# Encoder trunk on one core: first norm and first weight splits taken off GpSimd, and a scheduler that models transfers

## The chip, the core and the metric

The kernel runs on one core of one Trainium2 chip. Its engines run beside one another, each with its own queue, in order: TensorE (PE, matrix products, transposes by a product with the identity), VectorE (DVE), ScalarE (ACT), GpSimd (POOL) and SyncE (SP), which here issues all DMA transfers. The metric is the device time of one execution in microseconds; less is better.

## The reference

A trunk of two layers over 528 positions (16 meta tokens and 512 frames; pads in front stay zero), model width 1024, float32:

```python
for layer in range(DEPTH):
    hn = rms_norm(h, norm_g[layer])
    if layer % 2 == 0:   # A: sparse attention on top-k keys; B: gated linear attention
        out = layer_ab(hn, ...)
    else:                # C: retention with rotary; D: stick-breaking attention
        out = layer_cd(hn, ...)
    h = h + where(valid, out, 0)
return rms_norm(h[frames], final_g)

def rms_norm(x, g):
    return x * rsqrt(mean(x * x, -1) + 1e-6) * g
```

`layer_ab` begins with one projection of `hn` by `w_in_ab`, whose columns give the queries, keys, values and gates of A and B and the indexer (its queries IQ, its key, weights and B's low-rank gate); the indexer's scores pick 128 keys for each query. Each layer ends with a projection by `w_out_*`.

## The kernel before

Every float32 product is made from three products of split operands: an operand x is split into a high part (`hi`, written by ScalarE as fp32r) and the rest (`lo`, a subtraction, on VectorE). hh and hl are the split, normalised, transposed activations, 8 tiles of 128 features by 528 positions; wh and wl are a split weight tile, raw the tile as loaded (256 KB each, half of the rows of 128 columns). `products` issues hh x wh, hl x wh and hh x wl for each feature tile k, in two column halves of 272 (meta tokens and blocks 0 and 1) and 256 (blocks 2 and 3).

The head is `load_x` (lines 709 to 784). It loads the meta tokens (two halves x0 and x1 of 512 features, gv) and four blocks of 128 frames (x0 and x1, pt), the gains (mid) and five raw weights; IQ's two come first, then the two of the combined columns COMB (indexer key, indexer weights and low-rank gate, loaded in three pieces each into a zeroed tile). `square` adds up the squares, x0 on ScalarE and x1 on VectorE; `norm` makes the reciprocal root on ScalarE (`rstd`, two instructions) and scales x0 on VectorE and x1 on GpSimd (line 750). `turn` transposes one feature tile of a group of blocks on TensorE and writes hh (ScalarE, with the gain) and hl (VectorE). `split_next` (line 562) splits the next raw: of the first PW tiles the wh, and of the first PL tiles the wl, is GpSimd's (line 482: PW = 2, PL = 1). `consts` keeps TensorE at work before with 46 transposes of the identity.

No instruction goes straight to its engine. Each one is recorded (`Recorder.add`), with what it depends on and a cost in ns by `price`. `deadlines` then goes through all of them from the end and gives each the latest time at which it may begin for TensorE's order to hold; this is its priority (`pri`). `order` walks through time: on each engine, of the instructions that can start earliest, it takes the one with the least `pri`, and so sets the order of all five queues, and with it which buffers come free when. For VectorE it knows a collision: an instruction with both operands in SBUF (`port`) that starts while a GpSimd instruction runs is stretched to the end of that. A transfer's cost is a fixed 2000 and a share by its size, with any number of transfers side by side.

In the middle of the first layer the two head groups are worked between the projections: top-k (MAX and MATCH_REPLACE on VectorE over lt tiles of 272, 400 or 528 columns), GLA (st, vm, attm, the mask applied to the meta tokens' scores, used at lines 1324 to 1346), and softmax (wt, y).

Of the kernel before, what the change touches and what calls it, by code (L numbers as in the profile page):

```python
# [13 lines left out]
ALU = mybir.AluOpType  # L14
# [152 lines left out]
class Recorder:  # L167
# [48 lines left out]
    def price(self, o):  # L216
        o.mm, o.port = None, False
        n = max([x.free() for x in o.ins + o.outs] or [1])
        sbuf = not any(x.tile.psum for x in o.ins)
        scalar = 65 if any(isinstance(x, View) and x.free() == 1 for x in o.ins) and n > 1 else 0  # L220
        if o.eng == "tensor":
            lhs, rhs = (o.args[1], o.args[2]) if len(o.args) > 2 else (o.kw["lhsT"], o.kw["rhs"])
            turn = o.name == "transpose"
            plain = rhs.dtype == F32
            k, m, n = lhs.shape[0], lhs.free(), rhs.free()
            two = plain and not turn
            o.mm = (k, plain, max(n * 0.455 * (2 if two else 1) + 4, 107 * m / P + 4) + (107 if two and n <= P else 0))
            o.cost = max(273, 170 + 0.4375 * n) if not two else 180 + 1.62 * n
        elif o.eng == "scalar":
            o.cost = (205 if sbuf else 165) + 0.83 * n + (80 if isinstance(o.kw.get("bias"), View) or isinstance(o.kw.get("scale"), View) else 0)  # L230
            if "accum_out" in o.kw:
                o.cost += 200
        elif o.eng == "vector":
            o.port = sbuf and o.name not in ("max", "match_replace")
            if o.name == "tensor_tensor_scan":
                o.cost = 144 + 2.1 * n
            elif o.name in ("tensor_scalar", "tensor_copy") and sbuf:
                o.cost = 160 + 0.52 * n + scalar
            elif o.name == "memset":
                o.cost = 100 + 0.3 * n  # L240
            else:
                o.cost = 148 + 1.05 * n + scalar
            if o.name == "tensor_tensor_reduce" or "accum_out" in o.kw:
                o.cost += 80
            if o.name == "match_replace":
                o.cost += 70
        elif o.eng == "gpsimd":
            o.cost = {"memset": 92 + 0.84 * n, "tensor_tensor": 178 + 2.17 * n}.get(o.name, 194 + 1.5 * n)
        else:
            x = o.outs[0] if o.outs else o.ins[0]  # L250
            kb = n * x.shape[0] / 256
            o.cost = 2000 + kb * (9 if any(y.tile.whole for y in o.outs + o.ins) else 3.5)


    LAT = {"tensor": 55, "vector": 33, "scalar": 34, "gpsimd": 60, "sync": 27}
# [4 lines left out]
    def deadlines(self):  # L260


        ops, t, last = self.ops, 0.0, None
        due = {}
        for o in ops:
            if o.eng == "tensor":
                if last is not None:
                    t += self.slot(last, o)
                last = o
            due[o] = t  # L270
        late = {}
        turn = {}
        for o in reversed(ops):
            end = min([late[q] - self.LAT[q.eng] for q in o.succs] + [late[q] - self.LAT[q.eng] for x in o.tiles
                      for q in [turn.get((x.kind, x.at + x.kind.bufs))] if q and q.at > o.at], default=due[o] + 20000)
            start = end - o.cost
            if o.eng == "tensor":
                start = min(start, due[o])
            late[o] = start
            for x in o.tiles:  # L280
                turn[x.kind, x.at] = o
        for o in ops:
            o.pri = due[o] if o.eng == "tensor" else late[o]

    def order(self):
        ops = self.ops
# [5 lines left out]
        ends = {}  # L292
        free = dict.fromkeys(self.LAT, 0.0)
        lists = {e: [] for e in self.LAT}
        last = None
        begun = {}
        result = []

# [15 lines left out]
        while left:  # L314
            best = None
            for e, xs in lists.items():
                pick = None
                base = free[e] + (last.mm[2] if e == "tensor" and last is not None else 0)
                for o in xs:
                    est = o.est  # L320
                    ok = True
                    for t in o.tiles:
                        if t.slot:
                            continue
                        k = t.kind
                        if t.at != k.next or not k.free:
                            ok = False
                            break
                        est = max(est, min(k.free)[0] + self.LAT[e])
                    if not ok:  # L330
                        continue
                    now = free[e] + (self.slot(last, o) if e == "tensor" and last is not None else 0)
                    start = max(est, now)
                    key = (max(est + (self.MARGIN if e == "tensor" else 0) - base, 0.0), o.pri)
                    if pick is None or key < pick[0]:
                        pick = (key, start, o)
                if pick and (best is None or pick[1] < best[1]):
                    best = pick
            assert best, "no instruction can be placed"
            _, start, o = best  # L340
            e = o.eng
            lists[e].remove(o)
            cost = o.cost
            if e == "vector" and o.port and begun.get("pool", (0, 0))[0] < start < begun.get("pool", (0, 0))[1] - 100:
                cost += begun["pool"][1] - start - 70
            end = start + cost
            ends[o] = end
            o.begin, o.end = start, end
            if e == "tensor":
                free[e], last = start, o  # L350
            elif e == "sync":
                free[e] = start + 430
            else:
                free[e] = end + self.OVER[e]
                if e == "gpsimd":
                    begun["pool"] = (start, end)
# [40 lines left out]
class Kernel:  # L397
# [81 lines left out]
    LASTK = 4  # L479


    XL, XC, XN, XW, PW, PL = 2, 9, (0, 1, 1, 2), (1, 4, 7, 10, 13), 2, 1
    WARM = 46

    LAG = {"a": 5, "d": 6, "t": 1, "v": 4, "n": 9, "s": 6, "k": 11}
# [223 lines left out]
    def load_x(self):  # L709
        nc, ins = self.nc, self.ins  # L710
# [4 lines left out]
        for b in (None, 0, 1, 2, 3):  # L715
            n = NMETA if b is None else P
# [27 lines left out]
        def norm(b):  # L744
            n = NMETA if b is None else P
            x0, x1 = xs[b]
            r = ms[b][:n]
            self.rstd(r, r, DM)
            nc.vector.tensor_scalar(x0[:n], x0[:n], r, None, op0=ALU.mult)
            nc.gpsimd.tensor_scalar(x1[:n], x1[:n], r, 1.0, op0=ALU.mult, op1=ALU.mult)  # L750

        def turn(group, t0, k):
            tr = self.s()
# [13 lines left out]
        for b in first:  # L767
            square(b)
            norm(b)
# [640 lines left out]
    def out_ab(self):  # L1410
# [8 lines left out]
        rx = [self.wt() for _ in range(KT)]  # L1419
        halves = self.HALVES  # L1420
        begin = lambda f: self.begin(w, P * f, self.mh, self.ml, order=order)

        def residual(f):
# [369 lines left out]
```

## Time and profile before

| | |
|---|---|
| median of 3 runs | 663.05 us (662.98 to 663.65) |
| the profiled execution | 663.46 us |
| its span | 661.7 us |
| mean granted clock of TensorE | 0.984 |
| HBM traffic | 53.18 MB read, 6.90 MB written, 91 GB/s over the span |
| largest group of ScalarE, wh<-raw, x152 | 94.7 us, 629 ns each |
| largest group of VectorE, wl<-raw,wh, x153 | 109.1 us, 718 ns each |

Times in the profile are microseconds from the span's start. The span is what lies between the first and the last recorded instruction; the time of the execution has a little more around it. Idle time of an engine is put down to what ended it, in brackets as [time <- what]. A helper records every operation, so all have one line, L393 (in the changed kernel L403), and are told apart by tile names.

### The profile page before, as it was taken

To read this page: it belongs to the slowest core of one execution; us is meant where nothing else is said; L and a number is where in the kernel's file an instruction comes from. 1 tells how busy PE (TensorE), PEld (TensorE's weight loads), DVE (VectorE), ACT (ScalarE), POOL (GpSimd) and SP (SyncE) were. 2 spreads that over 40 slices of the span, in tenths; PEclk is the share of its full clock that TensorE was granted. 3 is DMA by queue.
4 is the path that set the end of the run, shared out by engine and by line. 5 is a ranking of instruction groups with operands and counts; after the bars stand their busy time and mean duration, and the time that the engine had idled before them with its cause. 6 is when DMAs were issued, how large, how long until landed. Compare 5 with 4: busy or idle time off the path is not lost.

```text
span 661.7 us, 12217 instructions
## 1 busy us (share of the span) xinstructions
PE 636.6 (96%) x4469; PEld 581.4 (88%) x4469; DVE 484.3 (73%) x1176; ACT 405.1 (61%) x910; POOL 76.4 (12%) x124
## 2 busy tenths in 40 slices
PE   5999999899999999999999999999999999999996
PEld 5879989798899999999899999878988888988884
DVE  4777799899987869679632764699935699955643
ACT  3656563353444877699643675799744699944434
POOL 7101110111000000001121110001200001110030
PEclk8899999799999999999999999999999999999998
DMA  7437222132322323112143272203322203224403
GB/s 217 118 83 224 72 74 72 46 96 65 81 57 75 98 65 97 52 47 65 50 145 112 67 238 81 64 21 93 97 65 64 78 2 104 83 71 149 153 17 127
DMA packets 91104, 59.25 MB, mean 90 GB/s; under 512 B 7315, under 2 KB 81629, under 8 KB 91045
## 3 DMA queue, kind: packets, MB, share of 16 engines
q1 hardware_dynamic: 91044, 58.48, 30.8%
q8 instruction: 35, 0.57, 0.3%
q14 instruction: 25, 0.20, 0.1%
HBM read 53.18 MB, written 6.90 MB: 91 GB/s over the span
## 4 chain that ended last, share of the span: by engine, by line
PE 67%; DVE 18%; ACT 9%; issue 2%; DMA 2%; SPq 0%; DVEq 0%; ACTq 0%
PE acc L393 45%; PE x L393 15%; PE y L393 6%; ACT wt L393 6%; DVE wt L393 5%; DVE st L393 3%; DVE lt L393 3%; DVE wl L393 3%; DVE m L393 2%; DMA pt<-in_x_dram 2%; ACT pt L393 1%; DVE pt L393 1%; ACT ptm L393 1%; ACT st L393 0%; DVE vt L393 0%
## 5 line engine op out<-in xcount | busy, mean ns | idle before, releaser
L393 PE MATMUL acc<-hh,wh 128*128 128x272 f32 (+2 forms) x968 | 246.5, 315 | 3.0 <-ACT hh L393 1.5
L393 PE MATMUL acc<-hh,wl 128*128 128x272 f32 (+2 forms) x968 | 234.2, 302 | 1.9 <-DVE wl L393 1.9
L393 PE MATMUL acc<-hl,wh 128*128 128x272 f32 (+2 forms) x968 | 234.8, 304 | 0.7 <-DVE hl L393 0.5
L393 ACT ACTIVATE wh<-raw 128x512 fp32r<-128x512 f32 x152 | 94.7, 629 | 125.2 <-PE acc L393 110.6
L393 PEld LDWEIGHTS acc<-hh,wh 128*128 128x128 f32 x968 | 159.5, 190 | 10.2 <-issue 3.0
L393 PEld LDWEIGHTS acc<-hh,wl 128*128 128x128 f32 x968 | 158.2, 190 | 8.5 <-DVE wl L393 2.8
L393 PEld LDWEIGHTS acc<-hl,wh 128*128 128x128 f32 x968 | 158.2, 190 | 5.0 <-DVE hl L393 1.5
L393 DVE TENSOR_TENSOR wl<-raw,wh 128x512 fp32r<-128x512 f32 x153 | 109.1, 718 | 57.2 <-ACT wh L393 52.2
L393 ACT ACTIVATE wt<-x 128x272 f32<-128x272 f32 (+3 forms) x100 | 43.0, 453 | 28.4 <-PE x L393 17.8
L393 POOL TENSOR_TENSOR gt<-gt,wt 128x528 f32<-128x528 f32 (+1 forms) x16 | 21.2, 1326 | 322.5 <-ACT wt L393 303.4
L393 PE MATMUL x<-st,st 128*128 128x272 f32 (+6 forms) x240 | 51.5, 292 | 0.1
L393 PE MATMUL x<-ident,wt 128*128 128x128 f32 (+2 forms) x300 | 46.0, 275 | 2.1 <-DVE wt L393 1.2
L393 ACT ACTIVATE wt<-wt 128x528 f32<-128x528 f32 (+3 forms) x74 | 42.9, 603 | 4.7 <-DVE wt L393 4.0
L393 PEld LDWEIGHTS x<-st,st 128*128 128x128 f32 (+2 forms) x240 | 37.5, 185 | 8.8 <-ACT wt L393 3.1
L393 ACT ACTIVATE wt<-wt,tiny 128x272 f32<-128x272 f32 (+5 forms) x64 | 34.7, 561 | 10.3 <-DVE tiny L393 10.0
L393 PEld LDWEIGHTS x<-ident,wt 128*128 128x128 f32 (+2 forms) x300 | 33.7, 139 | 7.0 <-DVE pt L393 1.4
L393 PE MATMUL y<-pt,vt 128*128 128x256 f32 (+1 forms) x288 | 38.6, 277 | 0.0
L393 PEld LDWEIGHTS y<-pt,vt 128*128 128x128 f32 x288 | 36.4, 189 | 1.3 <-DVE pt L393 0.7
L393 ACT ACTIVATE st<-acc 64x528 fp32r<-64x528 f32 (+1 forms) x58 | 34.7, 599 | 1.1 <-DVE lt L393 0.5
L393 DVE TENSOR_TENSOR_SCAN wt<-wt,wt 128x64 f32<-128x64 f32 (+5 forms) x50 | 30.8, 654 | 1.5 <-ACT wt L393 1.3
L393 DVE TENSOR_TENSOR pt<-x,pt 128x384 fp32r<-128x384 f32 (+1 forms) x48 | 28.1, 594 | 2.7 <-ACT pt L393 2.1
L393 ACT ACTIVATE wt<-wt,one 128x528 f32<-128x528 f32 (+3 forms) x42 | 29.5, 705 | 0.2
(191 smaller groups left out, 893.9 us busy)
## 6 DMA issues: line engine op xcount, KB each, us to landing
raw<-in_w_in_ab_dram SPq DMA_DIRECT2D x64, 256.0 KB, 2.8
raw<-in_w_in_cd_dram SPq DMA_DIRECT2D x56, 256.0 KB, 2.9
raw<-in_w_out_ab_dram SPq DMA_DIRECT2D x16, 256.0 KB, 2.8
raw<-in_w_out_cd_dram SPq DMA_DIRECT2D x16, 256.0 KB, 2.6
rep<-rows SPq DMA_DIRECT2D x8, 328.0 KB, 6.8
lt<-rep SPq DMA_DIRECT2D x8, 264.0 KB, 3.0
pt<-in_x_dram SPq DMA_DIRECT2D x8, 256.0 KB, 5.2
wt<-in_x_dram SPq DMA_DIRECT2D x8, 256.0 KB, 3.3
```

The lines of the kernel that those rows point to most:

```text
L393: getattr(getattr(self.core, o.eng), o.name)(*[bind(x) for x in o.args], **{k: bind(x) for k, x in o.kw.items()})
```

## The change

GpSimd's part of the first norm goes to VectorE, and the first two wh and the first wl go to ScalarE and VectorE (PW = PL = 0). The other parts are in the scheduler. A transfer now costs 3.6 ns per KB and takes its turn on one common wire: it ends when the wire is free, but not before 1900 ns after its issue, plus this cost; a transfer from DRAM to DRAM ends 6900 ns after its issue. Transfers get as priority the place at which the program asks for them (`o.at`) in place of the latest time, which is reckoned with 3000 ns more. And a GpSimd instruction that starts while a VectorE one with both operands in SBUF runs is stretched as well.

```diff
--- before.py
+++ after.py
@@ -249,7 +249,7 @@
         else:
             x = o.outs[0] if o.outs else o.ins[0]
             kb = n * x.shape[0] / 256
-            o.cost = 2000 + kb * (9 if any(y.tile.whole for y in o.outs + o.ins) else 3.5)
+            o.cost = kb * 3.6
 
 
     LAT = {"tensor": 55, "vector": 33, "scalar": 34, "gpsimd": 60, "sync": 27}
@@ -273,14 +273,14 @@
         for o in reversed(ops):
             end = min([late[q] - self.LAT[q.eng] for q in o.succs] + [late[q] - self.LAT[q.eng] for x in o.tiles
                       for q in [turn.get((x.kind, x.at + x.kind.bufs))] if q and q.at > o.at], default=due[o] + 20000)
-            start = end - o.cost
+            start = end - o.cost - (3000 if o.eng == "sync" else 0)
             if o.eng == "tensor":
                 start = min(start, due[o])
             late[o] = start
             for x in o.tiles:
                 turn[x.kind, x.at] = o
         for o in ops:
-            o.pri = due[o] if o.eng == "tensor" else late[o]
+            o.pri = due[o] if o.eng == "tensor" else o.at if o.eng == "sync" else late[o]
 
     def order(self):
         ops = self.ops
@@ -293,6 +293,7 @@
         free = dict.fromkeys(self.LAT, 0.0)
         lists = {e: [] for e in self.LAT}
         last = None
+        wire = 0.0
         begun = {}
         result = []
 
@@ -331,7 +332,8 @@
                         continue
                     now = free[e] + (self.slot(last, o) if e == "tensor" and last is not None else 0)
                     start = max(est, now)
-                    key = (max(est + (self.MARGIN if e == "tensor" else 0) - base, 0.0), o.pri)
+                    pri = o.pri
+                    key = (max(est + (self.MARGIN if e == "tensor" else 0) - base, 0.0), pri)
                     if pick is None or key < pick[0]:
                         pick = (key, start, o)
                 if pick and (best is None or pick[1] < best[1]):
@@ -343,13 +345,21 @@
             cost = o.cost
             if e == "vector" and o.port and begun.get("pool", (0, 0))[0] < start < begun.get("pool", (0, 0))[1] - 100:
                 cost += begun["pool"][1] - start - 70
+            if e == "gpsimd" and begun.get("port", (0, 0))[0] < start < begun.get("port", (0, 0))[1] - 100:
+                cost += begun["port"][1] - start - 100
             end = start + cost
+            if e == "vector" and o.port:
+                begun["port"] = (start, end)
             ends[o] = end
             o.begin, o.end = start, end
             if e == "tensor":
                 free[e], last = start, o
             elif e == "sync":
                 free[e] = start + 430
+                wire = end = max(wire, start + 1900) + o.cost
+                if o.outs and o.outs[0].tile.whole and o.ins and o.ins[0].tile.whole:
+                    end = start + 6900
+                ends[o] = o.end = end
             else:
                 free[e] = end + self.OVER[e]
                 if e == "gpsimd":
@@ -479,7 +489,7 @@
     LASTK = 4
 
 
-    XL, XC, XN, XW, PW, PL = 2, 9, (0, 1, 1, 2), (1, 4, 7, 10, 13), 2, 1
+    XL, XC, XN, XW, PW, PL = 2, 9, (0, 1, 1, 2), (1, 4, 7, 10, 13), 0, 0
     WARM = 46
 
     LAG = {"a": 5, "d": 6, "t": 1, "v": 4, "n": 9, "s": 6, "k": 11}
@@ -747,7 +757,7 @@
             r = ms[b][:n]
             self.rstd(r, r, DM)
             nc.vector.tensor_scalar(x0[:n], x0[:n], r, None, op0=ALU.mult)
-            nc.gpsimd.tensor_scalar(x1[:n], x1[:n], r, 1.0, op0=ALU.mult, op1=ALU.mult)
+            nc.vector.tensor_scalar(x1[:n], x1[:n], r, None, op0=ALU.mult)
 
         def turn(group, t0, k):
             tr = self.s()
```

What this does to the queues is shown at three places.

SyncE, the first transfers of the program (gv: meta tokens, pt: blocks of x, mid: gains, raw: weights). Before:

```order
1 L393 DMA pt_144<-in_x_dram 128x512
2 L393 DMA pt_157<-in_x_dram 128x512
3 L393 DMA pt_167<-in_x_dram 128x512
4 L393 DMA pt_177<-in_x_dram 128x512
5 L393 DMA gv_185<-in_meta_tokens_dram 16x512
6 L393 DMA gv_196<-in_meta_tokens_dram 16x512
7 L393 DMA raw_202<-in_w_in_ab_dram 128x4x128
8 L393 DMA mid_208<-in_norm_g_dram 16x128
9 L393 DMA mid_208<-in_gla_gate_b_dram 2x128
10 L393 DMA raw_224<-in_w_in_ab_dram 128x4x128
11 L393 DMA pt_234<-in_x_dram 128x512
12 L393 DMA raw_227<-in_w_in_ab_dram 128x4x64
```

Now:

```order
1 L403 DMA gv_144<-in_meta_tokens_dram 16x512
2 L403 DMA gv_157<-in_meta_tokens_dram 16x512
3 L403 DMA pt_167<-in_x_dram 128x512
4 L403 DMA pt_177<-in_x_dram 128x512
5 L403 DMA pt_185<-in_x_dram 128x512
6 L403 DMA pt_199<-in_x_dram 128x512
7 L403 DMA mid_207<-in_norm_g_dram 16x128
8 L403 DMA mid_207<-in_gla_gate_b_dram 2x128
9 L403 DMA raw_220<-in_w_in_ab_dram 128x4x128
10 L403 DMA raw_230<-in_w_in_ab_dram 128x4x128
11 L403 DMA pt_238<-in_x_dram 128x512
12 L403 DMA pt_250<-in_x_dram 128x512
```

The meta tokens stand ahead of the x blocks, both IQ weights (128x4x128) ahead of blocks 2 and 3, and the first piece of COMB (128x4x64) behind all of x, at row 15; its last two pieces (128x4x16), rows 23 and 27 before, are at rows 31 and 32.

ScalarE, its first instructions (wt, tiny: a square with its sum; tiny<-tiny: the two halves of a reciprocal root; wh: a weight's high part; hh: a transposed tile's high part). Before:

```order
6 L393 COPY gains<-x_257 128x18
7 L393 ACTIVATE wt_272,tiny_273<-pt_167 128x512
8 L393 ACTIVATE tiny_270<-tiny_270,eps 128x1
9 L393 ACTIVATE tiny_270<-tiny_270 128x1
10 L393 ACTIVATE wt_301,tiny_302<-pt_234 128x512
11 L393 ACTIVATE tiny_299<-tiny_299,eps 128x1
12 L393 ACTIVATE tiny_299<-tiny_299 128x1
13 L393 ACTIVATE wh_318<-raw_227 128x512
14 L393 ACTIVATE hh_327<-x_277,gains 128x272
15 L393 ACTIVATE hh_327<-x_279,gains 128x272
16 L393 ACTIVATE hh_327<-x_281,gains 128x272
```

Now:

```order
6 L403 ACTIVATE wt_264,tiny_265<-pt_185 128x512
7 L403 ACTIVATE tiny_262<-tiny_262,eps 128x1
8 L403 ACTIVATE tiny_262<-tiny_262 128x1
9 L403 COPY gains<-x_268 128x18
10 L403 ACTIVATE wh_285<-raw_220 128x512
11 L403 ACTIVATE tiny_289<-tiny_289,eps 128x1
12 L403 ACTIVATE tiny_289<-tiny_289 128x1
13 L403 ACTIVATE wh_298<-raw_230 128x512
14 L403 ACTIVATE wt_305,tiny_306<-pt_238 128x512
15 L403 ACTIVATE hh_316<-x_271,gains 128x272
16 L403 ACTIVATE hh_316<-x_275,gains 128x272
```

The wh ahead of the first hh was the first of COMB (raw_227); now the two of IQ stand there (raw_220, raw_230), and the wh of COMB are behind the thirteenth hh. The meta tokens' and block 0's squares and their roots, ahead of these rows, keep their order.

VectorE, in the top-k of the first layer (MAX and MATCH_REPLACE over lt; the wt<-y,tiny further on is a normalised attention output that TensorE transposes next). Before, with that wt at row 277:

```order
260 L393 MATCH_REPLACE lt_646<-m_35_1960,lt_646 128x400
261 L393 SCALAR_TENSOR_TENSOR st_1997<-st_1997,lt_1378,x_2029 64x128
262 L393 MATCH_REPLACE lt_635<-m_34_1930,lt_635 128x272
263 L393 SCALAR_TENSOR_TENSOR st_1997<-st_1997,lt_1378,x_2029 64x128
264 L393 MAX m_37_2137<-lt_635 128x8
265 L393 MAX m_38_2144<-lt_646 128x8
266 L393 MAX m_39_2151<-lt_687 128x8
267 L393 SCALAR_TENSOR_TENSOR st_2009<-acc_2058,wt_2027 64x4x64 x2
268 L393 SCALAR_TENSOR_TENSOR st_2023<-acc_2058,wt_2034 64x4x64 x2
269 L393 SCALAR_TENSOR_TENSOR st_2031<-acc_2058,wt_2027 64x4x64 x2
270 L393 SCALAR_TENSOR_TENSOR st_2041<-acc_2058,wt_2034 64x4x64 x2
```

Now, around that wt, at row 281:

```order
279 L403 TENSOR_REDUCE tiny_2195<-wt_2153 128x4
280 L403 TENSOR_TENSOR wl_2201<-raw_1867,wh_2144 128x512
281 L403 TENSOR_TENSOR wt_2210<-y_1930,tiny_2195 128x512
282 L403 TENSOR_TENSOR wl_2219<-raw_1937,wh_2185 128x512
283 L403 MAX m_38_2227<-lt_646 128x8
284 L403 MAX m_39_2238<-lt_687 128x8
285 L403 TENSOR_TENSOR mx_1934<-x_2225,gt_1921 128x512
286 L403 TENSOR_TENSOR wl_2255<-raw_2030,wh_2232 128x512
```

Before, all three MAX of this round (m_37, m_38 and m_39) stood ahead of it; now only m_37 does, at row 270, and the two of 400 and 528 columns (lt_646 and lt_687) come behind it. On the other hand the MAX of lt_646 of the round before (m_35), which stood at row 238, is now at row 260, still ahead of it.

Of GpSimd's rows eight go (two wh, one wl, five norms). VectorE gains six rows of these, ScalarE two. On TensorE no instruction is added or removed; rows move in the head and at some ten places behind it.

## The prediction

> **What bounds the kernel now.** I read the engines' shares and the granted clock in the page first, then TensorE's timeline for every idle stretch, then the chain and the timelines of the engines that TensorE waits for.
>
> ```profile
> span 661.7 us, 12217 instructions
> PE 636.6 (96%) x4469; PEld 581.4 (88%) x4469; DVE 484.3 (73%) x1176; ACT 405.1 (61%) x910; POOL 76.4 (12%) x124
> PEclk8899999799999999999999999999999999999998
> ```
>
> TensorE (PE) is busy for 96% of the span, so 661.7 - 636.6 = 25.1 us are idle. The matrix work isn't changed; time can come only from idle stretches or from stretches at a lower clock. The clock row has two low places, the first two slices (0 to 33 us) and the eighth (116 to 132 us). The profiled execution took 663.46 us, 1.76 more than its span. TensorE's timeline of the start, in order of time (start, length, what; in brackets the idle time before and who ended it):
>
> ```profile
> 1.59 7.31 PE L393 MATMUL y<-ident 128*128 128x128 f32 x46 [1.59 <-POOL ident masks.py:199]
> 9.63 0.35 PE L393 MATMUL x<-ident,gv 16*128 16x16 f32 x3 [0.57 <-DVE gv L393]
> 12.38 0.65 PE L393 MATMUL x<-ident,pt 128*128 128x128 f32 x3 [2.40 <-DVE pt L393]
> 14.96 0.90 PE L393 MATMUL x<-ident,pt 128*128 128x128 f32 x3 [1.93 <-DVE pt L393]
> 17.38 0.79 PE L393 MATMUL acc<-hh,wh 128*128 128x272 f32 x2 [1.52 <-ACT hh L393]
> 36.04 0.40 PE L393 MATMUL acc<-hh,wh 128*128 128x512 f32 x1
> ```
>
> After 46 warming transposes TensorE waits for VectorE's normalised x (pt) twice, and starts its first product at 17.38. 36.04 is the first product of the second column group, my mark for the end of the head. The clock in stretches (busy times of PE, PEld, DVE, ACT, POOL, then the clock, DMA share, GB/s):
>
> ```profile
> 12.00:13.00 1.00, 0.62 (x3) 0.31 (x3) 1.00 (x3) 0.09 (x1) 1.00 (x3) 0.84 1.11 349
> 13.00:22.00 9.00, 5.55 (x21) 4.13 (x20) 6.95 (x15) 5.23 (x14) 2.72 (x7) 0.50 0.80 191
> 22.00:23.00 1.00, 1.00 (x6) 0.96 (x7) 0.88 (x2) 0.23 (x1) 0.00 (x0) 0.54 0.00 0
> 23.00:36.00 13.00, 13.00 (x107) 12.64 (x107) 9.12 (x18) 8.16 (x18) 0.99 (x1) 1.00 0.31 78
> 122.00:128.00 6.00, 6.00 (x26) 5.02 (x26) 4.51 (x12) 0.76 (x3) 1.30 (x2) 0.50 0.18 44
> ```
>
> The clock is halved from about 12.7 to 22.9 (a mean of 0.84 from 12 to 13 and of 0.54 from 22 to 23), and again from 122 to beyond 128. It came back about 5.5 us after the products had begun at 17.38. What stands ahead of 17.38, by the chain of waits and by ScalarE's (ACT), VectorE's (DVE) and GpSimd's (POOL) timelines:
>
> ```profile
> 2.13 4.76 DMA pt<-in_x_dram
> ...
> 8.41 5.51 DMA pt<-in_x_dram
> ...
> 13.94 2.19 DMA raw<-in_w_in_ab_dram
> ...
> 16.23 0.63 ACT wh L393
> 16.86 0.39 ACT hh L393
> ```
> ```profile
> 7.14 0.63 ACT L393 ACTIVATE wt<-gv 16x512 f32<-16x512 f32 x1 [5.11 <-DMA gv<-in_meta_tokens_dram]
> 16.23 0.63 ACT L393 ACTIVATE wh<-raw 128x512 fp32r<-128x512 f32 x1 [2.79 <-DMA raw<-in_w_in_ab_dram]
> 10.34 1.99 DVE L393 TENSOR_SCALAR pt<-pt,tiny 128x512 f32<-128x512 f32 x1
> 13.48 1.43 DVE L393 TENSOR_SCALAR pt<-pt,tiny 128x512 f32<-128x512 f32 x1
> 19.34 1.15 DVE L393 TENSOR_SCALAR pt<-pt,tiny 128x512 f32<-128x512 f32 x1
> 23.70 0.48 DVE L393 TENSOR_SCALAR pt<-pt,tiny 128x512 f32<-128x512 f32 x1
> 16.89 0.69 DVE L393 TENSOR_TENSOR wl<-raw,wh 128x512 fp32r<-128x512 f32 x1 [1.32 <-ACT wh L393]
> 9.16 1.65 POOL L393 TENSOR_SCALAR gv<-gv,tiny 16x512 f32<-16x512 f32 x1 [0.65 <-DVE wt L393]
> 7.80 0.71 POOL L393 TENSOR_SCALAR wh<-raw 128x512 fp32r<-128x512 f32 x1 [1.02 <-DMA raw<-in_w_in_ab_dram]
> ```
>
> Three things hold the head. ScalarE and VectorE begin with the meta tokens (gv), which land at 7.1 behind four blocks of x. VectorE's norm takes 0.48 us at 23.70 and 1.15 to 1.99 us while GpSimd works. And ScalarE stands 2.79 us before a split of the combined weights (COMB), whose third piece of DMA lands at 16.13, with the first hh queued behind it.
>
> **The change part by part.**
>
> The norm and the splits. GpSimd loses eight instructions: five x1 norms, two wh, one wl. VectorE gains five norms of 0.48 us and one wl of 0.69, 3.1 us in all. In the head it is rid of the collisions, (1.99 - 0.48) + (1.43 - 0.48) + (1.15 - 0.48) = 3.1 us: VectorE's sum is even. TensorE's first transposes need x0 of the meta tokens and of blocks 0 and 1. Of the five x1 norms only that of the meta tokens stands ahead of the last of these on VectorE, together with the new wl; GpSimd's one of 16 rows took longer than those of 128, so I count it as a whole one, 0.5 us. The other four stand behind, between hl's. ScalarE gains two wh, 2 x 0.63 = 1.3 us, and loses the 2.79 us wait. For one norm on VectorE the bounds are 0.48 and 1.99; I take 0.48, since GpSimd has no norm or split any more that could run beside it, only memsets.
>
> The order of the transfers. SP now issues gv first, then all four x blocks, the gains, both IQ weights, blocks 2 and 3, and COMB's pieces last.
>
> ```profile
> 0.75 1.82 SPq L393 DMA_DIRECT2D pt<-in_x_dram  x4
> 2.61 0.89 SPq L393 DMA_DIRECT2D gv<-in_meta_tokens_dram  x2
> 3.55 0.42 SPq L393 DMA_DIRECT2D raw<-in_w_in_ab_dram  x1
> 18.47 0.96 SPq L393 DMA_DIRECT2D wt<-in_c_bucket_dram  x2
> ```
>
> One issue takes 0.45 us. The gv transfers are 32 KB each; a short one (the third piece above) took 2.19 from issue, so gv lands at about 3.0 and 3.4, and the four x halves of blocks 0 and 1 land 0.9 later, the last at 2.13 + 4.76 + 0.9 = 7.8. The first raw is the ninth transfer, issued at 0.75 + 8 x 0.45 = 4.35; it took 7.80 - 3.55 = 4.25 before, so it lands at 8.6. ScalarE's queue from 9.1 (when the warm-up has ended, at 1.59 + 7.31 = 8.9, and the gains are transposed) is gains 0.1, wh 0.6, rstd of block 1 0.5, wh 0.6, a square of block 2 with its read 0.75, and the first hh, 0.4 to 0.5. That gives hh at 12.1 and the **first product at about 12.3**, 5.1 earlier. VectorE's queue (wl 0.6 behind the first wh, then the norm of block 1, 0.5) lets the last transposes go at 11.2, so ScalarE ends last. Bounds: 11.5, if that square has its place before the splits, and 13.5, if the first raw takes the 5.51 us of the x transfer in the chain (9.9 instead of 8.6).
>
> From the first product to my mark TensorE has the same instructions: 17.38 to 22.7 at half clock, worth 2.7 at full, and 22.7 to 36.0 with no gap, 13.3. If the clock comes back 5.5 us after the first product again, at 17.8, the mark is at 17.8 + 13.3 = 31.1; I add 0.4 since both hl and wl for the first products now stand on VectorE: 31.5, so **-4.5** (-3.3 to -5.3 by the bounds of the first product). The cover is ScalarE and VectorE, at 5.23 and 6.95 of 9.00 us in the stretch above. COMB's products move to IQ's last quarter. From their first to the mark stand their 48 products and some nine of IQ, 0.12 us each (13.00 us for 107), 7.0 in all; with wh and wl before them, 1.3, its pieces may land until 31.5 - 8.3 = 23.2 without a wait. The last two are now SP's 31st and 32nd transfer; SP issued the 32nd and 33rd at 18.47, and with the 2.2 to 4.25 us of the two pieces of weights above they land at 20.7 to 22.7: hidden, by 0.5 us at least.
>
> [...]
>
> The places behind the head. Their rows:
>
> ```profile
> 92.65 0.51 PE L393 MATMUL acc<-hh,wh 128*128 128x272 f32 x2 [1.01 <-ACT wt L393]
> 121.71 0.22 PE L393 MATMUL x<-ident,st 64*16 64x64 f32 x1 [2.04 <-DVE attm L393]
> 168.38 0.81 PE L393 MATMUL x<-ident,wt 128*128 128x128 f32 x5 [1.17 <-DVE wt L393]
> 152.22 0.71 DVE L393 MAX8 m<-lt 128x8 f32<-128x528 f32 x1
> 160.84 1.53 DVE L393 MAX8 m<-lt 128x8 f32<-128x272 f32 x3
> 121.50 0.14 DVE L393 COPY_PREDICATED attm<-tri,x 16x16 f32<-16x16 int32 x1
> 322.83 0.65 PE L393 MATMUL x<-ident,wt 128*128 128x128 f32 x4 [0.53 <-DVE ptm L393]
> ```
>
> At 92.65 ScalarE's order changes and up to 0.9 us of the wait may go, but VectorE is full from 80 us to the attm at 121.50 and has the same work ahead of it; what TensorE gains it waits again at 121.71. TensorE now has three products more ahead of the transpose that waits there, three steps of 0.12 us: **-0.35**, bounds 0 and -1.0. The stretch at half clock behind it stays: over 6 us at half speed, 3.2 us lost. At 168.38 VectorE's wt comes late; of the three MAX of 160.84, those of 400 and 528 columns now stand behind it, and one of 400 comes in ahead: net the one of 528, 0.71 by the row of 152.22, so **-0.7**, bounds 0 and -1.17. Around 313 to 331 us and at 360, 375, 475 and 578 rows swap within their stretches; the longest wait there is 0.53, so I put 0, bounds -0.5 and +0.5.
>
> **Sum**: -4.5 - 0.35 - 0.7 = -5.5: 663.46 - 5.5 = 657.9 on the profiled execution. That one lay 0.41 above the median of 663.05, so **657.5** against the median.
>
> **The rivals.**
>
> - *The clock stays up in the head.* No idle stretch as long as 2.40 or 2.04 remains; against it, between 9.0 and 12.7 TensorE would still be busy for only some 1.5 us (two groups of transposes and the first product), and it had worked on after the wait at 121.71 when the clock fell. The head's 2.7 us lost at half clock come back, but hh and hl, 16 of each at about 0.4 us a step, then pace it: about 1.5 us more, 656.0. [...] Chance 0.10.
> - *The second drop goes too.* The wait at 121.71 falls on another phase. If the clock doesn't drop, 3.2 more: 654.3. Against it: the wait gets longer, not shorter. Chance 0.10.
> - *Half of the gain in the head is lost*: COMB's last pieces land after 23.2 and hh and hl queue behind their wh on ScalarE and wl on VectorE, as happens at 16.23 now with 2.79. Landing at 25.7, they cost 2.5: 660.0. Chance 0.12.
> - *The scheduler's model does nothing for the head*: the raw tiles or x land as late as now, since the same 16 DMA engines carry the same bytes (DMA share 0.80 to 1.11 there). Then 663, within 0.2%. Chance 0.05.
> - *Slower: VectorE starves TensorE and the clock stays down.* The products follow hl one by one, and VectorE has up to 3.1 us more to do if the long norms weren't long because of GpSimd. The clock returned with TensorE busy for 5.55 of 9.00 us; with less it might stay at 0.50. The mark then is at 12.3 + 2 x 16.0 = 44.3 if it stays for the whole head, 8.3 late. With a return at t half of t - 12.3 is done by then, and the mark is at t + 16.0 - (t - 12.3) / 2 = t / 2 + 22.15; it makes the kernel slower where that is over 36.04 + 1.05 (the two small terms), from t = 29.9. A return at 34 gives 663.05 + 34 / 2 + 22.15 - 37.09 = 665.1, and none before the mark 663.05 + 8.3 - 1.05 = 670.3. Chance 0.05.
>
> **How the numbers follow.** Forecast 0.58, its own range 656.0 to 659.4: the head's bounds with half of those of the small terms. With both rivals on the low side partly in, and the half gain in, 654.8 to 660.8 leaves out part of the second rival, the slower one and the unchanged one: 2 in 10. About 0.2% (1.3 us) is what a measurement can tell from no change. Faster by that: 0.58 + 0.10 + 0.10 + 0.12 = 0.90, less 0.02 for a half gain that is less than half: 0.88. Same: 0.06. Slower: 0.06.
>
> **What would show it.** First product near 12.3 (not 17.38), gv's square before 4, VectorE's pt norms all near 0.48, no wait of ScalarE for the COMB raw; the first 128x512 product near 31.5; the clock back near 18. Behind it every row 4.5 earlier, the 2.04 wait about 2 to 2.6 with its half clock, and 1.17 at the wt down to about 0.5. Wrong would be: a first product after 14, a wait of ScalarE or VectorE for raw near 22, norms still over 1 us, or a clock that returns after 20.

## The result, and the profile after

On one chip the changed kernel took 658.62 us in the median of 7 runs (657.29 to 661.0), the kernel before 663.65 in the median of 7 (662.98 to 665.36). The ratio is 0.9928, with a 95% interval of 0.9907 to 0.9949: 0.7% faster, 4.8 us by the ratio. The profiled execution took 661.0 us, at the slow end of the seven, with a span of 659.1. One execution among those below, the profiled one of e1, took 3451.54 us, with products some four times as long from end to end (1202 ns in the mean for acc<-hh,wh against 316 here), and is left out.

The page of the changed kernel, first lines and the clock:

```profile
span 659.1 us, 12207 instructions
PE 639.6 (97%) x4469; PEld 585.0 (89%) x4469; DVE 481.7 (73%) x1182; ACT 405.2 (61%) x912; POOL 68.7 (10%) x116
PEclk9799999699999999999999999999999999999998
```

TensorE's idle time went from 25.1 to 19.5 us, 5.6 less, but its busy time rose by 3.0: the same instructions spent more of it at half clock, where, from 13.56 to 23.80 of the changed kernel, 45 took 10.24 us, against 83 in the 9.98 us behind that, at a clock of 1.00 (rows of single steps, below, count those that run over a cut twice). TensorE's timeline of the head (start, length, what, idle time before):

```profile
1.58 7.74 PE L403 MATMUL y<-ident 128*128 128x128 f32 x46 [1.58 <-POOL ident masks.py:199]
11.40 0.55 PE L403 MATMUL x<-ident,pt 128*128 128x128 f32 x3 [0.95 <-DVE pt L403]
12.31 0.39 PE L403 MATMUL acc<-hh,wh 128*128 128x272 f32 x1 [0.36 <-ACT hh L403]
13.21 0.39 PE L403 MATMUL acc<-hl,wh 128*128 128x272 f32 x1 [0.50 <-DVE hl L403]
33.78 0.39 PE L403 MATMUL acc<-hh,wh 128*128 128x512 f32 x1
```

Of the waits of 2.40, 1.93 and 1.52 ahead of the first product the first is gone, the others are 0.95 and 0.36, and the product came at 12.31 instead of 17.38. A wait of 0.50 for hl, right behind it, is new. But the first 128x512 product, the end of the head, came only 2.26 us earlier. ScalarE's and VectorE's rows in the changed kernel:

```profile
2.55 0.63 ACT L403 ACTIVATE wt<-gv 16x512 f32<-16x512 f32 x1 [0.52 <-DMA gv<-in_meta_tokens_dram]
9.59 0.63 ACT L403 ACTIVATE wh<-raw 128x512 fp32r<-128x512 f32 x1
11.77 1.24 ACT L403 ACTIVATE hh<-x,gains 128x272 fp32r<-128x272 f32 x3
5.61 1.29 DVE L403 TENSOR_SCALAR gv<-gv,tiny 16x512 f32<-16x512 f32 x1
8.08 0.48 DVE L403 TENSOR_SCALAR pt<-pt,tiny 128x512 f32<-128x512 f32 x1
10.87 1.27 DVE L403 TENSOR_SCALAR pt<-pt,tiny 128x512 f32<-128x512 f32 x3
```

The meta tokens land near 2.5, the norms of 128 rows take 0.48 us, and ScalarE's queue from the gains to the first hh is as forecast. Only the norm of the meta tokens, at 5.61 beside GpSimd's memsets, is long, 1.29 us; it is off the path.

Where the rest of the head went is in the clock. Stretches of the kernel before (busy time of PE, PEld, DVE, ACT, POOL, then the clock, DMA share, GB/s), cut at the clock's changes:

```profile
9.27:12.68 3.41, 0.66 (x6) 0.56 (x6) 3.32 (x6) 1.61 (x6) 3.41 (x3) 1.00 0.92 238
12.68:16.09 3.41, 1.25 (x6) 0.51 (x4) 2.89 (x6) 0.50 (x2) 1.94 (x3) 0.50 0.80 160
16.09:19.51 3.42, 2.13 (x8) 1.68 (x8) 2.62 (x7) 3.25 (x9) 0.40 (x1) 0.50 0.80 208
19.51:22.92 3.41, 3.41 (x15) 2.83 (x15) 2.65 (x5) 1.73 (x5) 0.70 (x5) 0.50 0.60 170
```

and of the changed kernel, in the head and around the wait for attm:

```profile
10.15:13.56 3.41, 1.60 (x9) 0.92 (x8) 3.30 (x8) 2.83 (x9) 0.00 (x0) 1.00 1.14 346
13.56:16.97 3.41, 3.41 (x16) 2.53 (x14) 2.60 (x8) 1.91 (x6) 0.00 (x0) 0.50 0.96 238
16.97:20.39 3.42, 3.42 (x16) 2.84 (x15) 2.26 (x7) 1.42 (x5) 0.00 (x0) 0.50 0.38 50
20.39:23.80 3.41, 3.41 (x18) 3.41 (x17) 1.97 (x5) 1.43 (x3) 0.00 (x0) 0.50 0.00 0
23.80:33.78 9.98, 9.98 (x83) 9.92 (x83) 7.55 (x15) 6.92 (x14) 0.00 (x0) 1.00 0.50 129
115.97:119.38 3.41, 1.43 (x12) 1.13 (x10) 3.36 (x9) 2.81 (x5) 0.49 (x1) 1.00 0.32 77
119.38:122.79 3.41, 3.08 (x13) 2.63 (x13) 3.38 (x11) 0.00 (x0) 1.28 (x2) 0.50 0.27 64
122.79:126.21 3.42, 3.42 (x16) 2.79 (x15) 1.65 (x6) 0.76 (x3) 0.00 (x0) 0.50 0.04 13
126.21:129.62 3.41, 3.41 (x18) 3.41 (x17) 3.22 (x8) 0.63 (x1) 0.00 (x0) 0.50 0.01 3
```

In these two traces the low clock lasted a multiple of 3.41 us, called steps here: three in the head of both kernels (10.24 us), and at attm two before (121.92 to 128.74) and three after (119.38 to 129.62). Before, TensorE had little to do in the first two steps of the head (busy for 1.25 and 2.13 us); now all three were full (3.41, 3.42 and 3.41), so the same 10.24 us cost more work. The distance between the two falls is 109.24 us before and 105.82 after, 32 and 31 times 3.41 to within 0.12 us. In the changed kernel the clock fell after steps in which TensorE was busy for 1.60 and 1.43 of 3.41 us.

The time by stages, from the traces (e: the experiments below; the mark is the first 128x512 product, wt TensorE's transposes of the attention output at 168.38 before):

| trace | first product | at half clock in the head, then to wt | mark | mark to wt | wt to the end | span |
|---|---|---|---|---|---|---|
| before | 17.38 | 10.24, 6.83 | 36.04 | 132.34 | 493.32 | 661.7 |
| after | 12.31 | 10.24, 10.24 | 33.78 | 133.20 | 492.12 | 659.1 |
| e5, after again | 12.18 | 10.24, 10.24 | 33.63 | 133.12 | 492.25 | 659.0 |
| e2, scheduler only | 14.42 | 10.24, 3.41 | 34.86 | 131.06 | 492.28 | 658.2 |
| e3, late priority | 13.58 | 6.83, 6.83 | 33.77 | 132.06 | 492.27 | 658.1 |
| e11, norm and splits only | 13.60 | 10.24, 3.41 + 6.83 | 34.65 | 133.42 | 493.43 | 661.5 |
| e6, filled head | 11.70 | none, 3.41 | 28.79 | 131.19 | 492.32 | 652.3 |
| e9, filled twice | 11.78 | none, none | 28.85 | 131.79 | 492.36 | 653.0 |
| e10, filled head and e4's swap | 12.35 | none, 3.41 | 29.52 | 130.95 | 492.43 | 652.9 |

### The profile page after: what moved, and what is told of

It reads as the page before. It is cut to its first block, busy times and chain, and to the rows that moved or that the text cites. A ratio compares the mean times of both kernels' runs of the same rounds, so it can differ in the third digit from the quotient of the medians.

```text
span 659.1 us, 12207 instructions
## 1 busy us (share of the span) xinstructions
PE 639.6 (97%) x4469; PEld 585.0 (89%) x4469; DVE 481.7 (73%) x1182; ACT 405.2 (61%) x912; POOL 68.7 (10%) x116
## 4 chain that ended last, share of the span: by engine, by line
PE 75%; DVE 15%; ACT 6%; issue 2%; DMA 1%; SPq 0%; DVEq 0%; ACTq 0%
PE acc L403 51%; PE x L403 17%; PE y L403 7%; ACT wt L403 3%; DVE lt L403 3%; DVE st L403 3%; DVE wl L403 2%; DVE wt L403 2%; DVE m L403 2%; DMA pt<-in_x_dram 1%; ACT pt L403 1%; ACT st L403 1%; DVE pt L403 1%; DVE vt L403 0%; ACT ptm L403 0%
```

## The experiments

**e1 and e11: norm and splits alone, under the old scheduler.**

```diff
-            nc.gpsimd.tensor_scalar(x1[:n], x1[:n], r, 1.0, op0=ALU.mult, op1=ALU.mult)
+            nc.vector.tensor_scalar(x1[:n], x1[:n], r, None, op0=ALU.mult)
-    XL, XC, XN, XW, PW, PL = 2, 9, (0, 1, 1, 2), (1, 4, 7, 10, 13), 2, 1
+    XL, XC, XN, XW, PW, PL = 2, 9, (0, 1, 1, 2), (1, 4, 7, 10, 13), 0, 0
```

> The kernel before with the norm on VectorE and the first splits off GpSimd, under the old scheduler. Theory A (the head's gain comes from two causes, the GpSimd work and the order of the transfers, the latter with the meta tokens first and COMB's pieces last): the meta tokens still land near 7.1 us behind four x halves, the square of block 2 and its roots stand before the first hh, so the first product comes near 14.5 us, between 17.38 and 12.31, and the norms on VectorE take 0.48 us; time 660 to 662. Theory B (the collisions with GpSimd are the whole gain): first product at 12.3 to 12.8, time as the changed kernel, 657 to 660. On the clock: the stretches at half speed last a multiple of 3.41 us, whatever the kernel.

> The kernel of e1 once more, for its trace. By e1's times (1.5 us below the kernel before) theory A stands if the meta tokens land near 7.1 us, the norms take about 0.48 us, the first product comes at 14 to 15 us and ScalarE still stands before COMB's third piece near 16; theory B stands if the first product is at 12.3 to 12.8 and the gain is lost later.

e1: 661.92 us in the median of its nine other runs, ratio 0.9982 (0.9969 to 0.9995), 1.2 us. The timelines are e11's, the same kernel in one execution of 663.23 us; ScalarE, VectorE and TensorE:

```profile
7.19 0.63 ACT L393 ACTIVATE wt<-gv 16x512 f32<-16x512 f32 x1 [5.17 <-DMA gv<-in_meta_tokens_dram]
16.82 0.63 ACT L393 ACTIVATE wh<-raw 128x512 fp32r<-128x512 f32 x1 [2.51 <-DMA raw<-in_w_in_ab_dram]
10.73 0.47 DVE L393 TENSOR_SCALAR pt<-pt,tiny 128x512 f32<-128x512 f32 x1
13.60 0.59 PE L393 MATMUL acc<-hh,wh 128*128 128x272 f32 x1 [0.31 <-ACT hh L393]
34.65 0.47 PE L393 MATMUL acc<-hh,wh 128*128 128x512 f32 x1 [0.42 <-DVE st L393]
```

The norms are short and the first product comes 3.8 us earlier, 0.9 earlier than forecast, though the meta tokens still land at 7.2. Then ScalarE stands 2.51 us before COMB again, and 1.4 us are left at the mark. So the collisions were not the whole gain.

**e2: the scheduler alone** (the two lines above, the other way round, in the changed kernel).

> The changed scheduler alone; the norm's second half and the first splits stay on GpSimd. Theory A: the meta tokens land near 2.5 us, no wait of ScalarE for COMB, first product at 12.5 to 13.5 us, but the norms of blocks 0 and 1 on VectorE take over 1 us again beside GpSimd's; time 659 to 661, over half of the gain. Theory B (collisions are the whole gain): first product not before 16, time 662 to 664.

660.15 us in the median of 4 runs, ratio 0.9953 (0.9936 to 0.9969): 3.1 us, two thirds of the gain. VectorE's norm of block 1 is long again, and the first product comes later than the 12.5 to 13.5 forecast:

```profile
11.89 1.48 DVE L403 TENSOR_SCALAR pt<-pt,tiny 128x512 f32<-128x512 f32 x1
14.42 0.57 PE L403 MATMUL acc<-hh,wh 128*128 128x272 f32 x1 [0.45 <-ACT hh L403]
34.86 0.39 PE L403 MATMUL acc<-hh,wh 128*128 128x512 f32 x1
```

Only 1.2 us of its gain are in the head; 1.3 came from the stretch to wt, where the clock was low for one step instead of two, and 1.0 from behind wt. The two parts of the change nearly add: 1.2 + 3.1 = 4.3 of 4.8.

**e3: the latest time as a transfer's priority again.**

```diff
-            o.pri = due[o] if o.eng == "tensor" else o.at if o.eng == "sync" else late[o]
+            o.pri = due[o] if o.eng == "tensor" else late[o]
```

> The changed kernel with the latest time as a transfer's priority again, in place of its place in the program; wire model, 3000 ns of slack, collisions, norm and splits as changed. Theory A: the meta tokens are behind four x halves again and land near 7.1 us, the first product comes 1 us later than in the changed kernel, near 13.4; time 1 us above it, about 659.7, if the clock's phase is the same. Theory B (the program order of transfers gives nothing): first product at 12.3, the same time as the changed kernel.

659.87 us in the median of 4, ratio 0.9949 (0.9935 to 0.9964). ScalarE's and TensorE's rows:

```profile
6.73 0.63 ACT L403 ACTIVATE wt<-gv 16x512 f32<-16x512 f32 x1 [4.70 <-DMA gv<-in_meta_tokens_dram]
13.58 0.39 PE L403 MATMUL acc<-hh,wh 128*128 128x272 f32 x1 [0.44 <-ACT hh L403]
33.77 0.40 PE L403 MATMUL acc<-hh,wh 128*128 128x512 f32 x1
```

As theory A had it: the meta tokens 4 us later, the first product 1.3 us. The mark equals the changed kernel's, since the clock was low for two steps here and for three there.

**e8: the old cost of transfers, the program's order kept.**

```diff
-            o.cost = kb * 3.6
+            o.cost = 2000 + kb * (9 if any(y.tile.whole for y in o.outs + o.ins) else 3.5)
-            start = end - o.cost - (3000 if o.eng == "sync" else 0)
+            start = end - o.cost
-                wire = end = max(wire, start + 1900) + o.cost
-                if o.outs and o.outs[0].tile.whole and o.ins and o.ins[0].tile.whole:
-                    end = start + 6900
-                ends[o] = o.end = end
```

> The changed kernel with a transfer's cost as before (2000 and a share by size, side by side, no slack of 3000), its place in the program still its priority. Theory A (the wire model matters because it tells the scheduler that x lands early and the gains late: the square of block 1 goes ahead of the gains' copy): the square of block 1 and the splits now stand behind the gains' copy near 9.5 and its roots behind the square of block 2, so the first product comes at 14.5 to 15.0, and the time is 1 to 2 us above the changed kernel at the same clock. Theory B (the order by place in the program is all there is to it): the first product at 12.3 and the same time.

660.87 us in the median of 12, ratio 0.9955 (0.9942 to 0.9969), above the changed kernel on that chip (658.5 in e5) by 2.4 us in the medians and 1.8 by the ratios. TensorE's row:

```profile
13.45 0.59 PE L399 MATMUL acc<-hh,wh 128*128 128x272 f32 x1 [0.15 <-ACT hh L399]
```

Its profiled execution had a mean clock of 0.932, so no other time is taken from it. The first product was 1.1 us late, less than the 2.2 to 2.7 forecast, but late: the queue model is worth something by itself, through ScalarE's order (there the square of block 1 stands behind the gains).

**e5: the changed kernel again.**

> The changed kernel once more, on the chip of the next three. Theory A (the run-to-run spread of 657.3 to 661.0 us is the clock: stretches at half speed of 3.41, 6.83 or 10.24 us that begin and end on a grid of 3.41 us which stands otherwise in every run): the first product stays at 12.3 +- 0.3 and every order the same, the times go with the granted clock, about 3.7 us from 0.989 to 0.981, and the profiled run's stretches are again multiples of 3.41 us. Theory B (the spread is in transfers or engines): the first product or waits for DMA move by a microsecond, and times at one clock spread over 2 us.

658.5 us in the median of 6, ratio 0.9928 (0.9908 to 0.9948). The first product was at 12.18 and the waits are those of the first trace. Each run's time beside its mean granted clock, both sets of the changed kernel:

| clock | us |
|---|---|
| 0.981 to 0.982 | 661.0, 660.94, 660.71, 660.86 |
| 0.986 | 658.9, 658.62, 658.86 |
| 0.988 | 657.79, 658.04, 658.13, 658.14 |
| 0.989 | 657.29, 657.28 |

Times at one clock agree within 0.35 us. The spread of 3.7 us goes with the clock, as theory A has it. That doesn't hold for every kernel: the one before, run beside these, spread by 1.8 us at one clock (0.985, 662.41 to 664.18).

**e4: the wait for attm taken away.** The transpose of the meta tokens' keys goes ahead of the score product whose accumulator the mask's copy reads, and the products that use both come four steps later in place of one (`"t"` of LAG from 1 to 4).

```diff
+        self.transpose(m[:NMETA, 32:96], kh[0:64, :NMETA])
         nc.tensor.matmul(m[:NMETA, 0:16], ks[0:64, :NMETA], qs[0:64, :NMETA], start=True, stop=True)
         nc.vector.copy_predicated(attm, self.tri[:NMETA, :NMETA], m[:NMETA, 0:16])
-        self.transpose(m[:NMETA, 32:96], kh[0:64, :NMETA])
```

> The changed kernel with the transpose of the meta tokens' keys recorded ahead of their score product, so that it doesn't write the accumulator that the mask's copy still reads, and the products that use both four steps later instead of one. Theory A (the wait of 2.30 us for attm pulls the clock down, and this costs up to 5 us a time in the profiled run): the wait at 119.7 is below 0.5 us, no stretch at half clock between 115 and 132 us, time 3 to 6 us below the changed kernel, 653 to 656. Theory B (TensorE is behind VectorE there whatever is done): the wait moves to a later place of the same length and the clock still drops; time within 1 us of the changed kernel.

662.18 us in the median of 10, ratio 0.9976 (0.9959 to 0.9994): 3.2 us slower than the changed kernel by the ratios. The wait at 119.7 and the low clock there are gone, and in TensorE's timeline stand instead

```profile
130.44 0.49 PE L403 MATMUL y<-st,st 128*128 128x128 f32 x2 [1.72 <-DVE st L403]
132.74 0.78 PE L403 MATMUL y<-st,st 128*128 128x128 f32 x2 [1.46 <-DVE st L403]
```

with a lower clock behind them (1.00 up to 132.78, and 8 tenths in the clock row's slice from 132.1 to 148.6 us). Theory B's mechanism is seen: VectorE paces TensorE there, and the wait taken away at one place, 2.30 us, comes back as the two of 1.72 and 1.46 at the next. But theory B had the time within 1 us, and these waits aren't what was lost: counted by the products hh x wh done, the profiled execution was 0.6 us ahead of the changed kernel's near 210 us, and 1.7 us behind it from 350 to 430 us. The longer step changes the queues' order behind 300 us too; what cost the time there was not followed.

**e6 and e7: TensorE's waits in the head filled.** 16 transposes of x (8 of each of two blocks) into a buffer that nobody reads, ahead of the first product; e7 adds two for each of the first eight feature tiles.

```diff
         for g, t0, k, _ in todo[:self.XL]:
             turn(g, t0, k)
+        warm = self.pv()
+        for t in (xs[0][0], xs[1][0]):
+            for _ in range(8):
+                self.transpose(warm[:, :P], t[:, :P])
```

> The changed kernel with 16 more transposes (8 of a normalised tile of block 0, 8 of block 1, into a buffer that nobody reads) in TensorE's two waits ahead of the first product. Theory A (the clock falls because TensorE was busy for only 0.47 of the 3.41 us before 13.56): busy there goes to 0.9, the clock doesn't fall near 13.5, first product still before 12.7, first 128x512 product at 30 to 31.5 instead of 33.8, and 2 to 3 us less than the changed kernel at the same later stretches. Theory B (one window more or less of idle before makes no difference, the clock falls in the next window because hh and hl pace the products): it falls 3.4 us later, and the first 128x512 product comes within 0.7 us of 33.8.

> As the one before, with two more such transposes for each of the first eight feature tiles, placed where TensorE waits for hh and hl. Theory A: no stretch at half clock before 35 us, first 128x512 product at 30 to 31.5, 2 to 4 us below the changed kernel. Theory B: the transposes delay the products, about 16 x 0.11 = 1.8 us, and the first 128x512 product is at 33 or later.

e6: 656.06 us in the median of 5 (654.18 to 656.39), ratio 0.9885 (0.9867 to 0.9903), 2.4 us below the changed kernel on the same chip. e7: 656.49, ratio 0.9901 (0.9883 to 0.9919). Stretches of e6 in steps of 3.41 us, counted back from the fall of its clock at 116.96, and its mark:

```profile
7.74:11.15 3.41, 3.19 (x28) 2.66 (x26) 2.99 (x10) 2.34 (x7) 0.00 (x0) 1.00 1.00 315
11.15:14.57 3.42, 3.22 (x21) 2.27 (x19) 3.10 (x9) 2.38 (x9) 0.00 (x0) 1.00 1.05 301
14.57:17.98 3.41, 3.41 (x26) 3.03 (x26) 3.41 (x11) 2.82 (x9) 0.00 (x0) 1.00 0.93 204
113.55:116.96 3.41, 2.00 (x13) 1.55 (x14) 3.41 (x9) 0.26 (x1) 1.77 (x2) 1.00 0.05 4
```
```profile
28.79 0.39 PE L403 MATMUL acc<-hh,wh 128*128 128x512 f32 x1
```

With TensorE busy for 3.19 and 3.22 of 3.41 us the clock didn't fall in the head of the profiled execution, and the mark came 5.0 us before the changed kernel's, 0.6 of it ahead of the first product. At attm it fell after a step with 2.00 busy. By the two traces the low clock took 4.4 us of the head (33.78 - 12.31 against 28.79 - 11.70), some 1.5 a step, an estimate. Steps at nearly the same place ended differently: e10 below, with the head filled too, was busy for 3.08 us from 9.69 to 13.10 (counted back from its fall at 135.98) and the clock held behind that; e5 was busy for 1.61 us from 9.89 to 13.31, and there it fell. The profiled execution was the fastest of e6's five; three others had a mean clock of 0.989 against its 0.995, by an estimate two low steps more (0.006 of 652.3 us is 3.9, and a step at 0.50 takes 1.7 of it), at places that no trace shows. e7's clock held as well; its first product was 0.7 us later than e6's and its mark, at 30.31, 1.5 us: its further transposes delayed the products and brought nothing.

**e9 and e10: the filled head, and the wait at attm.** Both keep e6's filled head. e9 puts 16 more transposes, of the first GLA head's keys, ahead of the one that waits for attm; e10 makes e4's swap and leaves the step at one.

> The kernel with the 16 transposes in the head (e6) and 16 more of the first GLA head's keys, into a buffer nobody reads, ahead of the transpose that waits 2.30 us for attm. Theory A (each fall of the clock is lost time wherever it is): the clock doesn't fall between 110 and 130 us, and the time is 1 to 2 us below e6's 656.1, near 654.5. Theory B (behind that wait VectorE paces TensorE until 190 us, so a slow clock there costs little): no fall, or a later one, and the time within 0.7 us of e6's, the waits for st between 120 and 160 us longer by what the clock gave.

> The kernel with the 16 transposes in the head (e6) and the transpose of the meta tokens' keys recorded ahead of their score product, with the step to the products that use both left at one. Theory A (the wait comes from the transpose that writes the accumulator which the mask's copy still reads): the wait moves to the products with attm, five to eleven product rows later, and is 0.6 to 1.3 us shorter, 1.0 to 1.7; time 0.5 to 1.5 us below e6's. Theory B (VectorE is late and paces TensorE there): the wait is shorter by that, waits for st later are longer by as much, and the time stays within 0.5 us of e6's.

e9: 655.05 us in the median of 4, ratio 0.9873 (0.9857 to 0.9888). e10: 654.78 in the median of 5, ratio 0.9875 (0.9854 to 0.9897). TensorE's timeline of e9 around attm, then e10's wait:

```profile
112.10 1.97 PE L403 MATMUL x<-ident,st 128*128 128x128 f32 x16 [0.81 <-DVE wt L403]
114.79 0.22 PE L403 MATMUL x<-ident,st 64*16 64x64 f32 x1 [0.72 <-DVE attm L403]
117.21 0.43 PE L403 MATMUL x<-vm,mid 16*64 16x128 f32 x2 [0.54 <-DVE mid L403]
126.81 0.49 PE L403 MATMUL y<-st,st 128*128 128x128 f32 x2 [1.10 <-DVE st L403]
```
```profile
115.58 0.43 PE L403 MATMUL x<-vm,mid 16*64 16x128 f32 x2 [1.80 <-DVE attm L403]
```

In e9 the clock never fell before the kernel's tail (near 649.9, where TensorE has no work left), and its runs lie within 0.8 us; yet from the mark to wt it took 131.79, no less than with one low step (130.95 to 131.19), its 16 transposes of 1.97 us included. That speaks for theory B: TensorE waits for VectorE's st for 1.10 us at 126.81, where e6 has 0.22 at 126.17. The time alone doesn't decide, 0.8 us below e6's by the ratios, between the two forecasts. e10's wait became 1.80, not the 1.0 to 1.7 of theory A, and its clock fell once ahead of the tail, at 135.98. The intervals of e6, e9 and e10 overlap; that the second edit adds anything isn't shown. All three beat both kernels.

## Why the prediction was right, and where not

- **The first product.** Forecast 12.3, measured 12.31 and 12.18. Two of the three causes were put back one at a time: the collisions (e2, 2.1 us later) and the meta tokens behind x (e3, 1.3 us later). The third, ScalarE's stand before COMB, wasn't tried by itself; in e11 it comes at 16.82, behind the first product.
- **From there to the mark: the step that was mis-sized.** It put the clock's return 5.5 us after the first product, at 17.8, and the head at -4.5; a return after 20 stood in its own list of what would be wrong. In both profiled executions of the changed kernel the clock came back 11.4 and 11.5 us after it, at 23.5 and 23.8, and the head gained 2.26 and 2.41. The 5.5 was read as a time from the first product; it was what was left of 10.24 us that had begun at 12.68. The 0.4 added for VectorE is there, as the wait of 0.50 for hl. The other runs, up to 3.7 us faster at a higher clock, had fewer low steps somewhere; at 1.5 us a step in the head and about 1 to wt, two steps fewer than the profiled 661.0 make 658.5, which is an estimate for the median.
- **-0.35 at attm.** Not seen by itself: the wait went from 2.04 to 2.30. The price of 3.2 for this drop was too high: each step costs about 1 us between mark and wt (133.20, 132.06 and 131.06 for three, two and one), and for the last one e9 shows no gain, its transposes included.
- **-0.7 at wt: wrong.** The wait stayed at 1.20. VectorE had 0.5 us less MAX ahead of it, but the chain of st and acc that stands there waits for TensorE anyway, as this VectorE row shows:

```profile
151.13 0.85 DVE L403 SCALAR_TENSOR_TENSOR st<-acc,lt 64x256 f32<-64x256 f32 x2 [0.46 <-PE acc L403]
166.98 0.82 PE L403 MATMUL x<-ident,wt 128*128 128x128 f32 x5 [1.20 <-DVE wt L403]
```

  (The second row is TensorE's.) The MAX had filled gaps.
- **0 behind 313 us: from wt to the end it was -1.2.** The forecast looked at the waits around 320 us and put the swaps at 475 and 578 at nothing. Before, TensorE waits for pm at just these two places:

```profile
473.69 0.28 PE L393 MATMUL x<-ident,pm 128*32 128x128 f32 x1 [0.48 <-DVE pm L393]
577.19 0.28 PE L393 MATMUL x<-ident,pm 128*32 128x128 f32 x1 [0.47 <-DVE pm L393]
```

  In the changed kernel the same rows, at 471.70 and 574.68, have no wait. e11, under the old scheduler, has both (0.49 and 0.50), and 493.4 us behind wt; e2, e3 and e6 have neither, and 492.3. So this is the order that the new scheduler makes; which of its rules does it was not tried. A new wait for st, 0.58 at 187.16, stands against it.
- **The rivals.** COMB's pieces were not late: none of ScalarE's wh rows from 25.51 to 33.86 waits for a transfer. The clock staying up was priced at a mark of 30.0; e6's 17.1 us from the first product to the mark would make 29.4 from 12.31. The slower rival's middle did happen, a clock that came back at 23.8, short of its 29.9, but not by a starved TensorE: it was busy for 10.24 us of all three steps. Its sum for such a return, 23.8 / 2 + 22.15 = 34.05, is near the measured mark of 33.78.

The range held for the median, and in part by luck. Errors of both signs met: a head some 2 us smaller in the profiled executions, and 1.2 us behind wt that had been put at nothing. And on the profiled execution, for which the sum was made, 657.9 was forecast and 661.0 measured; that the median has fewer low steps nobody had forecast.

## What to carry to other kernels

Read the clock's low stretches by where they begin and end before using their length: in the head and at attm of the table's traces they lasted 3.41, 6.83 or 10.24 us from the fall, not a time from the first work. Work pulled into such a stretch was done at a clock of 0.50, so bringing the first product forward by 5 us brought its end forward by 2.3; 16 empty transposes ahead of it were worth another 2.4 us in the median. Where VectorE was the bound, a wait of TensorE taken away came back at the next place (e4: 2.30 us, then 1.72 and 1.46), and the step at full clock that e9 gained there brought no time.

## What was not expected of the hardware

The clock fell after steps in which TensorE was busy for a good part, 2.20 of 3.41 us in e2. The step ahead of the fall at attm in e2, and the only one at half clock behind it:

```profile
119.83:123.24 3.41, 2.20 (x15) 1.66 (x15) 3.41 (x11) 0.06 (x1) 1.77 (x2) 1.00 0.10 14
123.24:126.66 3.42, 3.42 (x17) 3.24 (x16) 2.69 (x8) 1.01 (x4) 0.00 (x0) 0.50 0.22 63
```

TensorE's busy time in the step before doesn't tell when it fell. In e10 the clock held behind the first of these steps, with 1.69 of 3.41 us busy, and fell behind the second, with 3.10:

```profile
112.09:115.50 3.41, 1.69 (x14) 1.48 (x12) 3.38 (x11) 2.42 (x5) 0.87 (x1) 1.00 0.28 71
132.57:135.98 3.41, 3.10 (x19) 2.02 (x19) 3.41 (x11) 3.35 (x7) 0.00 (x0) 1.00 0.00 0
```

In the first TensorE issued twelve products of 128x272 and then waited; the second has seven of 128x128, two of 128x272, and smaller ones for the rest. Whether this difference has to do with the fall was not tested. The clock came back after one step in e2 (TensorE busy for 3.42 us of 3.42), after two in e3's head (3.29 of 3.41 and 3.42 of 3.42), and after three in the changed kernel's (3.41, 3.42 and 3.41). What makes it one, two or three, no run here shows.
